# Seven-product f tiles of a SwiGLU half-FFN: three joins moved from VectorE into PSUM banks that ScalarE fills, and each tile's first product issued inside the tile before it

## The chip, the cores and the metric

The kernel is one program on one core of a Trainium2 chip. The metric is device time in microseconds (us) from the program's start to its end. The times of before are 2233.11 us as the median of three runs (2232.19 to 2233.71 us).

Five engines work side by side, each through a queue of its own in fixed order: TensorE (PE in the profile; its weight loads are PEld), VectorE (DVE), ScalarE (ACT), GpSimd (POOL) and SyncE (SP), which here issues nearly all DMAs. Matmuls write into PSUM, an accumulator memory that is used here as eight banks of 512 floats in each of 128 partitions. An engine's instruction that must wait holds up all that is behind it in the same queue.

## What is computed

The reference is one inference step of a two-layer network on 640 tokens (512 latent, 128 context) of width 1024. Each layer is a half-FFN, a token mixer (a Fourier mix in layer 0, attention in layer 1) and another half-FFN, each between norms that are modulated by a conditioning vector:

```python
m = (silu(cond) @ w_mod + b_mod).reshape(9, 1024)        # 9 rows of modulation for each layer
h = rmsnorm(x, g_pre) * (1 + m[3*k + 1]) + m[3*k]
gate, up = split(h @ w1, 2)                               # w1: 1024 x 5632
y = (silu(gate) * up) @ w2                                # w2: 2816 x 1024
x = x + 0.5 * m[3*k + 2] * rmsnorm(y, g_post)
```

There are four half-FFNs, numbered n = 0, 2, 3 and 5 among the six sub-layers. Every float32 product is done as three matmuls on a value split into a coarse part (`hi`) and the rest (`lo`): hi times hi, hi times lo, lo times hi.

## The kernel before

**f tiles.** A half-FFN walks over the 2816 hidden units in 22 tiles of 128, f = 0 to 21. Tile f needs 128 columns of gate weights and 128 columns of up weights over a depth of 1024 (eight chunks of 128), for two halves of the tokens (320 each). Tiles 0 to 3 are done plainly. Tiles 4 to 21 (`w1_fast`) use a scheme with seven products in place of eight blocks: (gate, up) x (first and second half of the depth) x (two token halves). One product is four chunks of three matmuls, 12 matmuls of 128x128 by 320 columns, written by `product`. Four of the seven read sums of activations that `combine` has prepared (`part(1..4)`), and some read sums of weights.

**Banks and joins of one tile.** The products go into four banks: x and y (`score`), z (`turn`) and w (`sum`), in the order x, y, z, w, then a second product on top of x, of z and of w. Between them seven VectorE instructions join the partial results: L715, L718, L722, L728, L729 (times the silu), L733 and L735; ScalarE copies x once (L712) and does the two silus (L725, L734). `hidden` splits each half of the result into hi and lo for the second layer of the FFN.

**Weights.** `unit(i)` hands out the i-th weight unit of a list and first sends every unit up to i + 3. `send` loads a unit by a DMA of 512 KB into a buffer named `raw` (four buffers, shared with everything that is loaded in this shape), then `split` makes hi on ScalarE (L220) and lo on VectorE (L221) in a pool of six pairs. For a fast tile the list has four units: `gate` (loaded), `sums` (the up weights are loaded, and three VectorE adds, L195 to L197, make the sums of gate and up), `up` (from the loaded up weights) and `all` (from the second half of the gate buffer, L203). A gate buffer is so in use until its tile's `all` unit has been split, and an up buffer until its `up` unit has been.

**The w2 stages.** After tiles 4, 8, 12, 16 and 21 a stage multiplies four (at the end six) finished tiles into the output: five token tiles, each 24 matmuls of 512 columns (`w2`). The sums are kept in SBUF between stages, so ScalarE copies each bank out (L781) and the next tile's in (L755). The stage holds its own four weight units to its end.

**Background work.** The modulation rows are matrix-vector products on VectorE: one job loads 512 KB of `w_mod_t` into a `raw` buffer and multiplies it with the two conditioning vectors (`gemv`, two instructions at L429). `behind` takes jobs off a list after each token tile of a w2 stage. `BEHIND` gives 36 jobs to each of n = 0, 2 and 3, which is 9 jobs in each of their four w2 stages, 12 stages in all, and 8 jobs to n = 5.

```python
BEHIND = (36, 12, 36, 36, 0, 8)
...
    def job(layer=layer, idx=idx, f=f):
        j = idx * NCH + f
        self.gemv(self.raw_tile(self.io["w_mod_t"][layer, j]), layer, j)
```

What sets the order on each queue is a scheduler that takes the program's order, priorities and free buffers and writes one fixed list for each engine.

Of the kernel before, what the change touches and what calls it, by code (L numbers as in the profile page):

```python
# [42 lines left out]
FAST = range(4, NF)  # L43
# [83 lines left out]
class Kernel:  # L127
# [54 lines left out]
    def send(self, kind, src):  # L182

        nc, two, one = self.nc, slice(512, UNIT), slice(0, 512)
        at = slice(0, UNIT)
        if kind in ("plain", "block", "gate"):
            raw = self.raw_tile(src)  # L190
            self.fast["gate"] = raw
        elif kind == "sums":
            up, gate = self.raw_tile(src), self.fast["gate"]
            raw = self.raw.tile([P, UNIT], F32, tag="raw", name=self.name("sums"))
            nc.vector.tensor_tensor(raw[:, one], gate[:, one], up[:, one], op=ALU.add)  # L195
            nc.vector.tensor_tensor(up[:, one], up[:, one], up[:, two], op=ALU.add)
            nc.vector.tensor_tensor(raw[:, two], gate[:, one], up[:, one], op=ALU.add)  # L197
# [12 lines left out]
        self.split(hi, lo, raw[:, at])  # L210
        return hi, lo
# [409 lines left out]
    def ffn(self, layer, which, base, boundary):  # L621
# [3 lines left out]
        n = layer * 3 + 2 * which  # L625
        begun = [False, False]
# [7 lines left out]
        def w1(fs, half):  # L634
# [4 lines left out]
            if n == half == 0 and 0 in fs:  # L639
                rest, pss = self.begun  # L640
                for go in rest:
                    go()
            elif len(fs) == 1:
                for f in fs:
                    for j in range(2):
                        with self.behind_of(*[] if n or half else (*self.entered, self.load)):
                            w = self.unit(base + self.w1_at[f] + j)
                        with self.tc.issue_after(self.latest.ins):
                            pss.append(self.proj(w, lambda k: k * P, half, kind="score" if f == 2 and n == 0 else "main"))
            else:  # L650
                pss = self.multi([self.unit(base + self.w1_at[f] + j) for f in fs for j in range(2)], half,
                                 ("main", "main", "turn", "sum"))
# [45 lines left out]
        def product(f, ps, unit, at, x, start):  # L698
            w = self.unit(base + self.w1_at[f] + unit)
# [4 lines left out]
        def w1_fast(f):  # L704

            g[f] = self.ring(F32R).rearrange("p (a t) -> p a t", a=2)
            a, q = (self.temp("left")[:, :HALF] for _ in range(2))
            s, v = (self.temp("right")[:, :HALF] for _ in range(2))
            x, y, z = (self.bank(kind)[:, :HALF] for kind in ("score", "score", "turn"))
            product(f, x, 0, 0, lambda k: self.h.chunk(k, 0), True)  # L710
            with high():
                nc.scalar.activation(a, x, AF.Copy)  # L712
            product(f, y, 1, 512, lambda k: part(2, k), True)
            with high():
                tt(q, y, a, op=ALU.subtract)  # L715
            product(f, z, 1, 0, lambda k: part(3, k), True)
            with high():
                tt(a, q, z, op=ALU.subtract)  # L718
            w = self.bank("sum")[:, :HALF]
            product(f, w, 2, 0, lambda k: part(1, k), True)  # L720
            with high():
                tt(a, a, w, op=ALU.add)  # L722
            product(f, x, 0, 512, lambda k: self.h.chunk(4 + k, 0), False)
            with high():
                nc.scalar.activation(s, x, AF.Silu)  # L725
            product(f, z, 2, 512, lambda k: part(4, k), False)
# [31 lines left out]
        def w2(s, tiles):  # L758
# [7 lines left out]
            for a0, f in [(a, f) for a in range(2) for f in range(f0, f1)] if ends else [(None, f) for f in range(f0, f1)]:  # L766
                w = self.unit(base + self.w2_at[s] + f - f0)
# [20 lines left out]
        for op, a, half in self.ffn_plan:  # L788
# [7 lines left out]
            elif op == "combine":  # L796
                combine(a)
            elif op == "fast":
                w1_fast(a)
# [8 lines left out]
            elif op == "gates":  # L808
                self.gate_rows(n)
                self.gates(n)  # L810
                if n % 3 == 0:
                    self.gate_rows(n + 1)
# [6 lines left out]
    def plan_ffn(self):  # L819

        plan = []
        for half in (0, 1):
            for i, fs in enumerate(((0, 1), (2,), (3,))):
                plan += [("w1", fs, half)]
                if half:
                    plan += [("combine", step, None) for step in ((), (0, 1), (2, 3))[i]]
        due = 0
        for f in FAST:
            if f == NF - 2:
                plan += [("gates", None, None)]  # L830
            plan += [("fast", f, None)]
# [5 lines left out]
        self.ffn_plan = plan  # L837
        self.ffn_units, self.w1_at, self.w2_at = [], {}, {}
        for op, v, half in plan:
            if op == "fast":  # L840
                self.w1_at[v] = len(self.ffn_units)
                self.ffn_units += [("gate", v, 0), ("sums", v, 1)]
                self.ffn_units += [(kind, None, None) for kind in ("up", "all")]
            elif op == "w1":
                for f in v:
                    if f not in self.w1_at:
                        self.w1_at[f] = len(self.ffn_units)
                        self.ffn_units += [("w1", f, 0), ("w1", f, 1)]
            elif op == "w2" and v[0] not in self.w2_at:
                self.w2_at[v[0]] = len(self.ffn_units)  # L850
                f0, f1 = SLICES[v[0]]
                self.ffn_units += [("w2", f0, j) for j in range(f1 - f0)]

    def list_units(self):
        io = self.io
        self.plan_ffn()
        self.bases = []
        for i in range(DEPTH):
            for sub in range(3):
                self.bases.append(len(self.units))  # L860
                if sub != 1:
                    for op, v, j in self.ffn_units:
                        if op == "w2":
                            self.units.append(("plain", io["w2"][i, sub // 2, v + j]))
                        elif op == "w1":
                            self.units.append(("block" if v == 3 else "plain", io["w1"][i, sub // 2, v, j]))
                        else:
                            self.units.append((op, None if v is None else io["w1"][i, sub // 2, v, j]))
# [598 lines left out]
```

## Time and profile before

| | before |
|---|---|
| median of three runs | 2233.11 us |
| profiled execution, its own time | 2233.16 us |
| its span, first to last instruction | 2231.4 us |
| mean granted TensorE clock | 0.996 |
| PE busy | 2198.5 us (99%) |
| DVE busy | 1682.5 us (75%) |
| ACT busy | 1155.6 us (52%) |
| DMA moved | 288.13 MB, mean 129 GB/s |

The page cuts the span into 40 slices: PE is at nine tenths or more in all but the first and the last. So only what makes PE wait can move the end, and the share of the other engines tells little by itself. Waits and the order of the queues have to be read stage by stage.

### The profile page before, as it was taken

The page shows a single profiled execution, that of the slowest core. Times are in us where ns is not written, and L with a number is a line of the kernel's source. Part 1 is how long each engine was busy: PE and PEld are TensorE (multiplying, and loading weights), DVE is VectorE, ACT ScalarE, POOL GpSimd, SP SyncE. Part 2 cuts the span into 40 slices and gives each one's busy share as a digit, 9 for nine tenths or more (in the row PEclk, how much of TensorE's full clock was granted, in tenths as well). Part 3 has the DMA queues.
Part 4 walks back from the last instruction along what each step waited for, and adds up shares of the span by engine and source line. Part 5 has one row for each costly group of instructions (what it writes and reads, how often), then busy time and mean ns, then how long its engine had stood idle before and what let it go on. Part 6 is the DMA issues. An engine that isn't in the chain of part 4 may idle for free. (4 is left out here: it accounts for less than half of the span.)

```text
span 2231.4 us, 35240 instructions
## 1 busy us (share of the span) xinstructions
PE 2198.5 (99%) x13730; PEld 2051.7 (92%) x13730; DVE 1682.5 (75%) x3081; ACT 1155.6 (52%) x2186; POOL 43.7 (2%) x95
## 2 busy tenths in 40 slices
PE   7999999999999999999999999999999999999998
PEld 5999999999899999998999999989999899999997
DVE  5888898687868898887688898776555666766684
ACT  4544454464544454455444554466878644455452
POOL 0000000010000000001000000000000000000000
PEclk8999999999999999999999999999999999999999
DMA  8144444432413444444144344523343322322232
GB/s 313 67 142 161 140 143 144 178 127 94 167 72 123 139 146 149 154 143 178 57 143 150 133 147 150 195 77 105 108 118 111 106 74 95 114 87 88 101 123 104
DMA packets 84424, 288.13 MB, mean 129 GB/s; under 512 B 9537, under 2 KB 14497, under 8 KB 84129
## 3 DMA queue, kind: packets, MB, share of 16 engines
q1 hardware_dynamic: 83712, 285.23, 37.6%
q8 instruction: 107, 1.75, 0.3%
q10 hardware_dynamic: 544, 0.66, 0.1%
q14 instruction: 61, 0.49, 0.1%
HBM read 270.34 MB, written 11.58 MB: 126 GB/s over the span
## 5 line engine op out<-in xcount | busy, mean ns | idle before, releaser
L220 ACT ACTIVATE hi<-raw 128x1024 fp32r<-128x1024 f32 (+1 forms) x374 | 358.4, 973 | 330.2 <-PE score L235 86.9
L221 DVE TENSOR_TENSOR lo<-raw,hi 128x1024 fp32r<-128x1024 f32 (+1 forms) x374 | 416.0, 1118 | 142.1 <-ACT hi L220 140.9
L234 PE MATMUL main<-hi,ring 128*128 128x512 f32 (+2 forms) x1044 | 391.4, 375 | 0.0
L235 PE MATMUL main<-lo,ring 128*128 128x512 f32 (+2 forms) x1044 | 387.8, 372 | 0.8 <-DVE lo L221 0.8
L236 PE MATMUL main<-hi,ring 128*128 128x512 f32 (+2 forms) x1044 | 387.2, 371 | 0.0
L429 DVE SCALAR_TENSOR_TENSOR junk<-raw,wide 128x1024 bf16<-128x1024 f32 x256 | 313.1, 1223 | 95.7 <-DMA raw<-in_w_mod_t 91.3
L236 PE MATMUL score<-ring,lo 128*128 128x320 f32 x896 | 277.1, 309 | 0.3 <-DVE lo L221 0.3
L234 PE MATMUL score<-ring,hi 128*128 128x320 f32 x896 | 277.4, 310 | 0.0
L235 PE MATMUL score<-ring,hi 128*128 128x320 f32 x896 | 276.9, 309 | 0.0
L234 PEld LDWEIGHTS main<-hi,ring 128*128 128x128 f32 x1044 | 196.3, 188 | 34.9 <-issue 1.7
L235 PEld LDWEIGHTS main<-lo,ring 128*128 128x128 f32 x1044 | 196.3, 188 | 33.8 <-DVE lo L221 1.1
L236 PEld LDWEIGHTS main<-hi,ring 128*128 128x128 f32 x1044 | 196.1, 188 | 33.9 <-issue 0.2
L234 PE MATMUL turn<-ring,hi 128*128 128x320 f32 x648 | 200.5, 309 | 2.3 <-DVE left L718 2.1
L236 PE MATMUL sum<-ring,lo 128*128 128x320 f32 x648 | 200.2, 309 | 0.0
L235 PE MATMUL sum<-ring,hi 128*128 128x320 f32 x648 | 200.2, 309 | 0.0
L234 PE MATMUL sum<-ring,hi 128*128 128x320 f32 x648 | 200.2, 309 | 0.0
L235 PE MATMUL turn<-ring,hi 128*128 128x320 f32 x648 | 200.2, 309 | 0.0
L236 PE MATMUL turn<-ring,lo 128*128 128x320 f32 x648 | 200.2, 309 | 0.0
L781 ACT ACTIVATE y<-main 128x512 f32<-128x512 f32 x160 | 94.2, 591 | 200.0 <-PE main L236 199.0
L234 PE MATMUL main<-ring,hi 128*128 128x320 f32 x560 | 181.8, 325 | 1.6 <-ACT ring L220 1.6
L235 PE MATMUL main<-ring,hi 128*128 128x320 f32 x560 | 174.9, 312 | 0.8 <-DVE ring L221 0.8
L236 PE MATMUL main<-ring,lo 128*128 128x320 f32 x560 | 174.8, 312 | 0.0
(247 smaller groups left out, 4371.4 us busy)
## 6 DMA issues: line engine op xcount, KB each, us to landing
raw<-in_w SPq DMA_DIRECT2D x264, 512.0 KB, 3.9
raw<-in_w_mod_t SPq DMA_DIRECT2D x128, 512.0 KB, 3.5
raw<-in_qkv SPq DMA_DIRECT2D x26, 512.0 KB, 3.8
first<-in_w_mod_k SPq DMA_DIRECT2D x16, 512.0 KB, 8.8
spill<-ring SPq DMA_DIRECT2D x12, 640.0 KB, 2.9
ring<-spill SPq DMA_DIRECT2D x12, 640.0 KB, 7.2
raw<-in_bias SPq DMA_DIRECT2D x16, 448.0 KB, 3.8
raw<-in_four_in SPq DMA_DIRECT2D x8, 512.0 KB, 3.8
```

The costliest lines, as they stand in the source:

```text
L220: a = self.nc.scalar.activation(hi, src, AF.Copy)
L221: self.last_split = a, self.nc.vector.tensor_tensor(lo, src, hi.bitcast(F32), op=ALU.subtract)
L234: mm(out, whi, xhi, start=start, stop=False)
L235: mm(out, whi, xlo, start=False, stop=False)
L236: self.latest = mm(out, wlo, xhi, start=False, stop=stop)
L429: last = self.nc.vector.scalar_tensor_tensor(out=self.junk, in0=raw, scalar=1.0, in1=self.wide[:, cond, :], op0=ALU.mult, op1=ALU.mult, ac ...
L781: nc.scalar.activation(place(i, a), ps[a], AF.Copy)
```

## The change

Only `w1_fast`, the list of units and their planning change (`EARLY` is 4, so the branches for another value never run, and `first_half` is never called). Four things are different for tiles 5 to 21 of each half-FFN (tile 4 runs much as before):

- ScalarE puts minus x into bank y before the y product, which then accumulates on top; it copies y into bank w before the w product, which accumulates on top as well; it copies z and y to SBUF. So the joins L715, L718 (in its old place), L722 and L733 become one subtraction (new L765), and four joins are left: L765, L793, L794, L804. ScalarE has six instructions here for three before.
- The tile's products are issued as z, y, second x, w, then the next tile's first x product (`open_fast`), then second z and second w. In tiles 20 and 21 y goes ahead of z.
- The list of units has the next tile's `gate` ahead of this tile's `all`, so the gate weights of a tile are loaded in the tile before it.
- The second of two `gate_rows` calls, each a transposition on PE through bank `turn`, moves from ahead of tile 20 to ahead of tile 21.

```diff
-        elif kind == "sums":
-            up, gate = self.raw_tile(src), self.fast["gate"]
+            if kind == "gate":
+                self.fast["next"] = raw
+        elif kind in ("sums", "again"):
+            self.fast["gate"] = self.raw_tile(src[0]) if kind == "again" else self.fast.pop("next")
+            up, gate = self.raw_tile(src[1]), self.fast["gate"]
...
+        def open_fast(f):
+            if f is None or f in opened:
+                return
+            opened.append(f)
+            product(f, held["x"], "gate", 0, chunk(0, 0), True)
...
+            steps = {
+                "y": lambda: product(f, y, "sums", 512, parts(2), not seeded),
+                "z": lambda: product(f, z, "sums", 0, parts(3), True),
+            }
+            if seeded:
+                with high():
+                    copy(y, x, AF.Copy, scale=-1.0)
+                a, q = left(), left()
+                for step in ("yz" if turned else "zy"):
+                    steps[step]()
+                    with high():
+                        if step == "z":
+                            copy(a, z, AF.Copy)
+                        else:
+                            w = self.bank("sum")[:, :HALF]
+                            copy(w, y, AF.Copy)
+                            copy(q, y, AF.Copy)
+                product(f, x, "gate", 512, chunk(4, 0), False)
+                s, v = right(), q
+                with high():
+                    copy(s, x, AF.Silu)
+                product(f, w, "up", 0, parts(1), False)
+                with high():
+                    tt(a, w, a, op=ALU.subtract)
...
+            open_fast(ahead)
+            product(f, z, "up", 512, parts(4), False)
             with high():
                 tt(v, q, z, op=ALU.subtract)
                 tt(v, v, s, op=ALU.mult)
                 hidden(f, v, 0)
-            product(f, w, 3, 0, lambda k: self.h.chunk(4 + k, 1), False)
+            product(f, w, "all", 0, chunk(4, 1), False)
             with high():
-                nc.vector.scalar_tensor_tensor(out=q, in0=w, scalar=-1.0, in1=q, op0=ALU.mult, op1=ALU.subtract)
-                nc.scalar.activation(q, q, AF.Silu)
+                if seeded:
+                    q = left()
+                    copy(q, w, AF.Silu, scale=-1.0)
                 tt(a, a, q, op=ALU.mult)
                 hidden(f, a, 1)
...
+                need(v, "sums", "again" if again else "sums")
+                need(v, "up")
+                if half[0] is not None:
+                    need(half[0], "gate")
+                need(v, "all")
```

How the queues change is shown at one w2 stage, the second of n = 0, which stands between tiles 8 and 9; the other eleven stages with nine background jobs read alike. First SyncE's loads around the stage, as they stood before. `raw_1769` is the stage's last w2 unit, `raw_1781` and `raw_1793` are gate and up of tile 9, the `in_w_mod_t` rows are the background jobs, and `raw_1995` is the gate of tile 10.

```order
L172 DMA raw_1769<-in_w 128x1024
L172 DMA raw_1781<-in_w 128x1024
L172 DMA raw_1793<-in_w 128x1024
L172 DMA raw_1821<-in_w_mod_t 128x1024
L172 DMA raw_1853<-in_w_mod_t 128x1024
```

Now, on the same queue: `raw_1625` is the gate of tile 9, loaded ahead of the stage's four w2 units, `raw_1792` is the up of tile 9, and `raw_1818` is already the gate of tile 10.

```order
L172 DMA raw_1625<-in_w 128x1024
L172 DMA raw_1700<-in_w 128x1024
L172 DMA raw_1719<-in_w 128x1024
L172 DMA raw_1753<-in_w 128x1024
L172 DMA raw_1780<-in_w 128x1024
L172 DMA raw_1792<-in_w 128x1024
L172 DMA raw_1818<-in_w 128x1024
L172 DMA raw_1832<-in_w_mod_t 128x1024
L172 DMA raw_1864<-in_w_mod_t 128x1024
```

One load more, the gate of tile 10, has moved ahead of the background loads. Next VectorE at the end of the same stage, before. `lo_1810` and `lo_1979` are the `up` and `all` weights of tile 9, which can be split only when the stage's weights come free; L429 are the background jobs, L715 and L718 joins of tile 9.

```order
L429 SCALAR_TENSOR_TENSOR junk,mod<-raw_1929,wide 128x1024
L221 TENSOR_TENSOR lo_1810<-raw_1793,hi_1809 128x1024
L429 SCALAR_TENSOR_TENSOR junk,mod<-raw_1929,wide 128x1024
L442 TENSOR_TENSOR coef<-mod,vec 128x8
L221 TENSOR_TENSOR lo_1979<-raw_1781,hi_1978 128x512
L442 TENSOR_TENSOR coef<-mod,vec 128x8
L429 SCALAR_TENSOR_TENSOR junk,mod<-raw_1961,wide 128x1024 x2
L429 SCALAR_TENSOR_TENSOR junk,mod<-raw_1965,wide 128x1024
L715 TENSOR_TENSOR left_1971<-score_1975,left_1970 128x320
L429 SCALAR_TENSOR_TENSOR junk,mod<-raw_1965,wide 128x1024
L718 TENSOR_TENSOR left_1970<-left_1971,turn_1976 128x320
```

Now, at the same place (`lo_1809` is `up` and `lo_1987` is `all` of tile 9, `lo_1821` the gate of tile 10, L765 a join of tile 9); two more jobs, `raw_1972` and `raw_1976`, come behind the rows shown, and only behind them the adds that make the sums of tile 10.

```order
L431 SCALAR_TENSOR_TENSOR junk,mod<-raw_1900,wide 128x1024
L223 TENSOR_TENSOR lo_1809<-raw_1792,hi_1808 128x1024
L223 TENSOR_TENSOR lo_1821<-raw_1818,hi_1820 128x1024
L431 SCALAR_TENSOR_TENSOR junk,mod<-raw_1900,wide 128x1024
L223 TENSOR_TENSOR lo_1987<-raw_1625,hi_1986 128x512
L431 SCALAR_TENSOR_TENSOR junk,mod<-raw_1904,wide 128x1024 x2
L431 SCALAR_TENSOR_TENSOR junk,mod<-raw_1936,wide 128x1024 x2
L765 TENSOR_TENSOR left_1983<-sum_2015,left_1983 128x320
L431 SCALAR_TENSOR_TENSOR junk,mod<-raw_1940,wide 128x1024 x2
L444 TENSOR_TENSOR coef<-mod,vec 128x8 x2
```

Of the stage's 18 background instructions 5 stood behind the `up` split of tile 9 before; now 11 do. Last PE where tile 10 first needs its sums (`hi_2034`, `lo_2035` before). Before, that is the y product, behind the first x product (`score_2106`):

```order
L234 MATMUL score_2106<-ring_212,hi_1997 128x320
L235 MATMUL score_2106<-ring_213,hi_1997 128x320
L236 MATMUL score_2106<-ring_212,lo_1998 128x320
L234 MATMUL score_2107<-ring_824,hi_2034 128x320
L235 MATMUL score_2107<-ring_825,hi_2034 128x320
L236 MATMUL score_2107<-ring_824,lo_2035 128x320
```

Now the sums (`hi_2038`, `lo_2039`) are needed by the z product (`turn_2111`), behind the second x product (`score_910`), and the y product (`score_911`) is woven into it:

```order
L236 MATMUL score_910<-ring_336,hi_1820 128x320
L237 MATMUL score_910<-ring_337,hi_1820 128x320
L238 MATMUL score_910<-ring_336,lo_1821 128x320
L236 MATMUL turn_2111<-ring_893,hi_2038 128x320
L237 MATMUL turn_2111<-ring_894,hi_2038 128x320
L236 MATMUL score_911<-ring_824,hi_2038 128x320
L237 MATMUL score_911<-ring_825,hi_2038 128x320
L238 MATMUL turn_2111<-ring_893,lo_2039 128x320
```

From the end of the stage to this point PE has eight products before (seven of tile 9 and the first x of tile 10) and eight now (z, y, second x and w of tile 9, the first x of tile 10, second z and second w of tile 9, the second x of tile 10).

More of the change, by code (lines that the diff above doesn't have):

```diff
@@ L650, in w1 @@
             else:
-                pss = self.multi([self.unit(base + self.w1_at[f] + j) for f in fs for j in range(2)], half,
+                pss = self.multi([self.unit(base + w1_at[f, kind]) for f in fs for kind in ("gate", "up")], half,
                                  ("main", "main", "turn", "sum"))
@@ new lines, in ffn, with first_half @@
+        chunk = lambda c, half: lambda k: self.h.chunk(c + k, half)
+        parts = lambda i: lambda k: part(i, k)
+        copy = nc.scalar.activation
+        stash, held, opened = {}, {}, []
+        def first_half(fs):
+            room = self.ring(F32).rearrange("p (i t) -> p i t", t=HALF)
+            pss = [self.bank()[:, :HALF] for _ in fs]
+            stash.update({f: (room[:, 2 * i], room[:, 2 * i + 1]) for i, f in enumerate(fs)})
+            for i, f in enumerate(fs):
+                product(f, pss[i], "gate", 0, chunk(0, 0), True)
+                with high():
+                    copy(stash[f][0], pss[i], AF.Copy)
+            for i, f in enumerate(fs):
+                product(f, pss[i], "gate", 512, chunk(4, 0), False)
+                with high():
+                    copy(stash[f][1], pss[i], AF.Silu)
@@ new lines, in open_fast, with w1_fast @@
+        def open_fast(f):
[3 more added lines that the diff above has]
+            product(f, held["x"], "gate", 0, chunk(0, 0), True)
+        def w1_fast(f, ahead, turned):
+            g[f] = self.ring(F32R).rearrange("p (a t) -> p a t", a=2)
+            if not held:
+                held.update({kind: self.bank("score")[:, :HALF] for kind in "xy"})
+            seeded = bool(opened)
+            x, y = held["x"], held["y"]
+            z = self.bank("turn")[:, :HALF]
+            left, right = (lambda kind=kind: self.temp(kind)[:, :HALF] for kind in ("left", "right"))
+            steps = {
[17 more added lines that the diff above has]
+                s, v = right(), q
+                with high():
+                    copy(s, x, AF.Silu)
+                product(f, w, "up", 0, parts(1), False)
+                with high():
+                    tt(a, w, a, op=ALU.subtract)
+            else:
+                if f in stash:
+                    b, s = stash.pop(f)
+                else:
+                    open_fast(f)
+                    b, s = left(), right()
+                    with high():
+                        copy(b, x, AF.Copy)
+                q = left()
+                steps["y"]()
+                with high():
+                    tt(q, y, b, op=ALU.subtract)
+                steps["z"]()
+                a, v = left(), right()
+                with high():
+                    tt(a, q, z, op=ALU.subtract)
+                w = self.bank("sum")[:, :HALF]
+                product(f, w, "up", 0, parts(1), True)
+                with high():
+                    tt(a, a, w, op=ALU.add)
+                if opened:
+                    product(f, x, "gate", 512, chunk(4, 0), False)
+                    with high():
+                        copy(s, x, AF.Silu)
+            open_fast(ahead)
+            product(f, z, "up", 512, parts(4), False)
```

116 lines of the change are left out of this document (60 added, 56 removed).

## The prediction

> **What bounds the kernel now.** I read the page first, busy shares and slices, then the list of waits by length, then the windows around a w2 stage, and last the timelines of VectorE and PE there.
>
> ```profile
> PE 2198.5 (99%) x13730; PEld 2051.7 (92%) x13730; DVE 1682.5 (75%) x3081; ACT 1155.6 (52%) x2186; POOL 43.7 (2%) x95
> ```
>
> PE is busy for 2198.5 of 2231.4 us, and the change leaves the number of matmuls as it is. So it can only win what PE waits today, and lose what PE will wait. The waits in the seven-product tiles are these:
>
> ```profile
> PE turn L538 <- ACT rms L540: 2.7, 2, 1.5
> PE turn L234 <- DVE left L718: 2.1, 2, 1.4
> PE score L236 <- DVE lo L221: 0.3, 1, 0.3
> ```
>
> L538 is the transposition of `gate_rows`, L718 a join, the third the split of a tile's sums. Together 5.1 us: that is all the change can gain, 0.2% of the span. What it can lose stands in the tightest place of a half-FFN, the w2 stage with background jobs and the four tiles behind it (window: busy time of PE, PEld, DVE, ACT, POOL, then clock):
>
> ```profile
> 181.80:209.00 27.20, 27.20 (x122) 22.54 (x121) 21.63 (x36) 13.72 (x23) 0.00 (x0) 1.00 0.43 146
> 209.00:258.30 49.30, 49.30 (x337) 49.26 (x337) 46.83 (x77) 24.59 (x38) 0.00 (x0) 1.00 0.43 144
> ```
>
> PE fills both windows, but VectorE is at 46.83 of 49.30 us behind the stage: it has hardly any room to work off a backlog. Nine jobs, 18 background instructions (each with a short read, so two records), fall to this place:
>
> ```profile
> 181.80:209.00 27.20, 16.01 (x26) 1.00 0.43 146
> 209.00:221.40 12.40, 6.14 (x10) 1.00 0.56 190
> ```
>
> That is L429 alone: 13 of 18 run inside the stage, 5 behind it.
>
> **Part 1, the joins.** 68 tiles (17 in each of four half-FFNs) lose three VectorE instructions each and gain three ScalarE copies.
>
> ```profile
> L728 DVE TENSOR_TENSOR right<-left,turn 128x320 f32<-128x320 f32 x72 | 34.7, 482 | 4.2 <-PE turn L236 4.1
> L712 ACT ACTIVATE left<-score 128x320 f32<-128x320 f32 x72 | 31.0, 430 | 10.3 <-PE score L236 9.3
> ```
>
> VectorE: 204 x 0.482 = 98 us less. ScalarE: 204 x 0.430 = 88 us more; in four tiles 12 x 0.43 = 5.2 on top of 24.6 of 49.3, so there is room. Neither shortens PE's own work; both are worth only the waits above, at most the 2.1 of L718. No row of before shows a 320-column copy into PSUM at a join; the nearest, of 512 columns, take 602 ns into PSUM and 591 out of it, so I price it as the 0.43 out.
>
> ```profile
> L755 ACT ACTIVATE main<-y 128x512 f32<-128x512 f32 x146 | 87.6, 602 | 15.3 <-DVE ring L583 11.0
> L781 ACT ACTIVATE y<-main 128x512 f32<-128x512 f32 x160 | 94.2, 591 | 200.0 <-PE main L236 199.0
> ```
>
> The copy into bank y has z's product in front of it, the copy into w the second x product, so nearly all are covered. A product is 12 matmuls at a pitch of 0.147 us, 1.76 us:
>
> ```profile
> 302.00 0.31 PE L234 MATMUL turn<-ring,hi 128*128 128x320 f32 x1
> 302.15 0.31 PE L235 MATMUL turn<-ring,hi 128*128 128x320 f32 x1
> ```
>
> Where that cover fails is rival two. Behind the last join, L793 to L804, stand 1.76 us of PE's next product: 0 for each tile, 0.6 at most.
>
> **Part 2, the gate unit loaded a tile earlier.** This is where I expect the time to go. Of four `raw` buffers, before, two are held through the stage (gate and up of tile 9) and two circulate for the jobs. Now gate 9, up 9 and gate 10 are all loaded ahead of the jobs and all held, since up 9 cannot be split before the stage's weights leave the pool and gate 10 stays until its `all`. One buffer is left: each job's load must wait for the second L429 (L431 now) of the job before it. What such a round costs is seen on VectorE:
>
> ```profile
> 188.42 0.08 DVE L429 DVE_READ_ACCUMULATOR junk<-raw,wide 128x1 f32 x1
> ...
> 192.07 1.23 DVE L429 SCALAR_TENSOR_TENSOR junk<-raw,wide 128x1024 bf16<-128x1024 f32 x1 [2.97 <-DMA raw<-in_w_mod_t]
> ...
> 194.61 1.23 DVE L429 SCALAR_TENSOR_TENSOR junk<-raw,wide 128x1024 bf16<-128x1024 f32 x1
> ...
> 197.03 0.08 DVE L429 DVE_READ_ACCUMULATOR junk<-raw,wide 128x1 f32 x1
> ...
> 200.82 1.23 DVE L429 SCALAR_TENSOR_TENSOR junk<-raw,wide 128x1024 bf16<-128x1024 f32 x1
> ```
>
> The job that reads until 188.50 frees a buffer whose next content is read from 192.07: 3.57 us. Again 197.11 to 200.82: 3.71. So a round is 3.65, and a job's two instructions 2.54 (192.07 to 194.61), together 6.2 us for each job, where two buffers gave 13 instructions in the stage.
>
> In us from the stage's start (181.8), the length 27.2 as before. The split of the sums of tile 9, which has to come first, waits for PE's last product, some 0.8 later than its 183.78 today; the first load goes at 4.0, so the first four jobs start at 7.65, 13.85, 20.05 and 26.25. In VectorE's list the first half of the fourth job ends at 27.5; then follow the splits of up 9 and gate 10 (28.65 and 29.8), the fourth job's second half (31.1) and the half split of `all` (31.7). These free three buffers at 28.7, 31.1 and 31.7, and jobs 5, 6, 7 have data 3.65 later, 32.3, 34.8, 35.4. From 32.3 VectorE is full: five jobs x 2.54 = 12.7, four joins 1.6, coefficients 0.2, two ring splits 0.8 (by L728's spacing of 0.4). The last background instruction ends at **47.5**; before, at 34.7:
>
> ```profile
> 183.78 1.22 DVE L221 TENSOR_TENSOR lo<-sums,hi 128x1024 fp32r<-128x1024 f32 x1
> ...
> 216.41 0.08 DVE L429 DVE_READ_ACCUMULATOR junk<-raw,wide 128x1 f32 x1
> ...
> 218.03 0.69 DVE L195 TENSOR_TENSOR sums<-raw,raw 128x512 f32<-128x512 f32 x1
> ...
> 219.75 0.69 DVE L197 TENSOR_TENSOR sums<-raw,raw 128x512 f32<-128x512 f32 x1
> ...
> 221.57 1.23 DVE L221 TENSOR_TENSOR lo<-sums,hi 128x1024 fp32r<-128x1024 f32 x1 [0.40 <-ACT hi L220]
> ...
> 223.11 1.22 DVE L221 TENSOR_TENSOR lo<-raw,hi 128x1024 fp32r<-128x1024 f32 x1
> ```
>
> All 18 stand in VectorE's list ahead of the adds of tile 10's sums: three adds 2.1 (49.6), hi on ScalarE 1.06 (50.7), lo 1.22 (51.95).
>
> ```profile
> L220 ACT ACTIVATE hi<-sums 128x1024 fp32r<-128x1024 f32 x72 | 76.4, 1061 | 123.7 <-DVE sums L197 111.5 <-PE sum L235 10.0 <-DVE right L728 1.4
> ```
>
> PE has eight products to its first matmul on these sums: 27.2 + 8 x 1.76 + 0.2 for a join = 41.5. It waits 50.7 - 41.5 = **9.2 us**, and 0.1 more for lo. Before, its y product stood at 41.3 with lo ready at 41.0 (222.8): the margin was 0.3, so the backlog is paid in full. Queued behind the waiting matmul is PE's whole list, so nothing covers it.
>
> **The clock after such a wait.** The last matmul of the program starts at 2224.67; the clock reads 1.00 for 3.6 us and 0.50 behind. At the start the long wait ends at 35.94 with the clock at 0.50 until 41:
>
> ```profile
> 2224.67 0.39 PE L236 MATMUL main<-hi,ring 128*128 128x512 f32 x1
> 2225.20:2228.80 3.60, 0.00 (x0) 0.00 (x0) 2.18 (x4) 0.64 (x2) 0.54 (x1) 1.00 0.12 46
> 2229.00:2231.40 2.40, 0.00 (x0) 0.00 (x0) 0.00 (x0) 0.00 (x0) 0.00 (x0) 0.50 0.32 119
> 35.94 0.64 PE L234 MATMUL main<-ring,hi 128*128 128x320 f32 x1
> 37.17 0.47 PE L235 MATMUL main<-ring,hi 128*128 128x320 f32 x1
> 37.44 0.47 PE L236 MATMUL main<-ring,lo 128*128 128x320 f32 x1
> 34.20:40.90 6.70, 6.05 (x31) 5.17 (x28) 2.00 (x8) 2.09 (x6) 0.00 (x0) 0.50 1.03 378
> 41.00:47.00 6.00, 6.00 (x43) 6.00 (x43) 3.93 (x11) 5.97 (x9) 0.00 (x0) 1.00 0.75 304
> ```
>
> So a wait of 9.2 us, over 3.7, drops the clock, and PE then runs about 5.0 us (35.94 to 41) at a pitch of 0.267 in place of 0.147: 5.0 x (1 - 0.147/0.267) = 2.25 us lost.
>
> The Trainium skill ("TensorE: Matmul & The Clock Gate", section "The HAM clock gate") has the clock fall after an idle window of about 3.4 us and rise again after about 3.4 us of busy time. By that figure, an estimate, a stall would lose 1.5 us, and the sum be 2358. The rows agree with the fall (3.7 us) and show a longer way back (5.0).
>
> **The sum.** 9.2 + 2.25 + 0.1 = 11.6 us for a stage. The same list stands at all 12 stages with nine jobs (four each in n = 0, 2, 3): 139 us. The four stages of n = 5 have two jobs each, done by 7.65 + 6.2 + 2.54 = 16.4 with the stage still running, and cost nothing. Less the 5.1 of waits that go: +134. The profiled execution took 2233.16 us, 1.8 over its span and equal to the median of 2233.11: 2233 + 134 = **2367 us**.
>
> Bounds for a stage. Low: a round of 3.3 instead of 3.65 (the loads land in 3.5 by the page's median, part of a round) ends the jobs 1.7 earlier; with joins and splits lying inside the waits for data, 1.6 earlier again; no clock loss: 5.9, so 12 x 5.9 - 5 = +66, 2299.
>
> ```profile
> raw<-in_w_mod_t SPq DMA_DIRECT2D x128, 512.0 KB, 3.5
> ```
>
> High: first load 2 us later, half clock through all 6.7 us of its window (3.0), 0.7 of backlog left for tile 11: 9.2 + 2 + 3.0 + 0.7 = 14.9, less 5: +174, 2407.
>
> **The rivals.** *As aimed* (6%): the jobs keep pace, so that no new wait comes and all 5.1 us go: 2228. It decides by whether nine jobs still end by about 34.7. For it speaks that VectorE has 98 us less to do; against it that those are 1.2 us for a tile, while the loop through one buffer lacks 12.8.
>
> *The copies into bank w come late, and the backlog doesn't* (9%): in the second tile behind each of 16 stages only four matmuls (0.59 us) lie between the y product's end and the w product. The copy needs 0.16 for the last matmul's end (0.31 long at a pitch of 0.147) and 0.43, 0.59 in all, so just enough, or up to 1.06 more when a hi split is ahead on ScalarE. 16 x 0 to 1.06 = 0 to 17 us, less 5: 2228 to 2245. It needs the jobs to end in time, like the first.
>
> *The backlog is handed on* (4%): VectorE's spare 2.5 us behind a stage don't absorb what remains, so that tiles 11 and 12 wait as well: over 2407.
>
> That the change does not do what it says is excluded by the lists: the three joins are gone and the gate load stands ahead.
>
> **How the numbers follow.** The backlog has 81%, of it nearly all between its bounds. The range is 2299 to 2407; both small rivals and the long one are left out. 0.2% (4.5 us) is about what a measurement of this kernel tells from no change. Faster is the first rival and the near end of the second, 0.07; same is most of what is left of the second, 0.05; slower the rest, 0.88.
>
> **What would show it.** The background instructions wait for DMA before nearly every job in the stages; PE waits about 9 us, 12 times, in the second tile behind a stage (tiles 6, 10, 14, 18) at bank `turn` for hi of the sums; the clock reads below 1.00 just behind it; the four tiles behind a stage take 61 us, not 49.3; VectorE's busy time falls by some 98 us. Wrong it would be if these waits are absent, if two loads of `w_mod_t` overlap in a stage, or if n = 5 loses as much as n = 0.

## The result, and the profile after

The changed kernel takes 2359.92 us (median of five runs, 2357.02 to 2363.33) against 2233.11 us before: a ratio of 1.0568, 95% interval 1.0553 to 1.0584. The prediction was 2367 us, with a range of 2299 to 2407. The profiled execution has a span of 2359.5 us, 128.1 more than before.

The page of the changed kernel, the row of busy times (microseconds, share of the span, instructions), then of the 40 slices PE's busy tenths and its clock:

```profile
PE 2232.1 (95%) x13730; PEld 2075.4 (88%) x13730; DVE 1608.9 (68%) x2877; ACT 1225.3 (52%) x2390; POOL 43.7 (2%) x95
PE   7989889899999889889998898899999999999998
PEclk8999999999999999999999999999999999999999
```

VectorE does 73.6 us less, ScalarE 69.7 more, PE has the same 13730 matmuls and is busy 33.6 us longer. The slices at 8 show that PE now waits in the first two thirds, where n = 0, 2 and 3 lie. The list of waits names the place (what waited and for what; us in total, times, longest). First VectorE's loads before, then the changed kernel:

```profile
DVE junk L429 <- DMA raw<-in_w_mod_t: 91.3, 54, 3.7
```

```profile
DVE junk L431 <- DMA raw<-in_w_mod_t: 208.9, 75, 4.5
PE turn L236 <- ACT hi L222: 98.3, 12, 8.6
PE turn L540 <- DVE left L793: 1.0, 1, 1.0
PE turn L236 <- DVE left L793: 0.7, 1, 0.7
```

Twelve waits of 8.2 us in the mean, on the split of a tile's sums, at bank `turn`; and the background instructions waited 208.9 us for their loads, where they had waited 91.3. The row names ScalarE, since its hi came last; what held hi up is found by following VectorE back. PE's other idle time is 3.8 us shorter on balance (2231.4 - 2198.5 = 32.9 us before, 2359.5 - 2232.1 - 98.3 = 29.1 now): 98.3 + 33.6 - 3.8 = 128.1.

VectorE's timeline at the second w2 stage of n = 0, which starts at 194.6 in this run (start, length, engine and line, tiles; in brackets the idle time before and what ended it):

```profile
202.00 1.22 DVE L431 SCALAR_TENSOR_TENSOR junk<-raw,wide 128x1024 bf16<-128x1024 f32 x1 [3.12 <-DMA raw<-in_w_mod_t]
...
208.03 1.23 DVE L431 SCALAR_TENSOR_TENSOR junk<-raw,wide 128x1024 bf16<-128x1024 f32 x1 [3.54 <-DMA raw<-in_w_mod_t]
...
214.05 1.23 DVE L431 SCALAR_TENSOR_TENSOR junk<-raw,wide 128x1024 bf16<-128x1024 f32 x1 [3.51 <-DMA raw<-in_w_mod_t]
...
220.19 1.23 DVE L431 SCALAR_TENSOR_TENSOR junk<-raw,wide 128x1024 bf16<-128x1024 f32 x1 [3.64 <-DMA raw<-in_w_mod_t]
...
241.60 0.08 DVE L431 DVE_READ_ACCUMULATOR junk<-raw,wide 128x1 f32 x1
241.60 0.68 DVE L197 TENSOR_TENSOR sums<-raw,raw 128x512 f32<-128x512 f32 x1
...
244.85 1.22 DVE L223 TENSOR_TENSOR lo<-sums,hi 128x1024 fp32r<-128x1024 f32 x1 [0.40 <-ACT hi L222]
```

That is one job each 6.0 us, with a wait of 3.5 us for the load before each: one buffer goes round. The sums of tile 10 (L197) come right behind the last background instruction. The same time on PE: the stage and the four tiles behind it as two windows (busy time of PE, PEld, DVE, ACT, POOL; the clock), then PE alone in three parts of the second:

```profile
194.60:221.80 27.20, 27.20 (x122) 22.54 (x121) 13.29 (x22) 14.61 (x24) 0.00 (x0) 1.00 0.32 97
221.80:282.80 61.00, 52.45 (x337) 51.35 (x337) 50.22 (x78) 28.01 (x49) 0.00 (x0) 0.92 0.41 138
```

```profile
236.40:244.80 8.40, 0.00 (x0) 0.69 0.32 112
244.90:249.70 4.80, 4.80 (x17) 0.50 0.34 109
249.80:282.80 33.00, 33.00 (x224) 1.00 0.38 128
```

PE stands still for 8.4 us, then works 4.8 us at half clock: 17 matmuls in 4.8 us, which take 17 x 0.147 = 2.5 at full clock, so 2.3 us are lost. The four tiles take 61.0 us, not 49.3. This stage has the longest of the twelve waits; the shortest is 7.2 us.

| us from the stage's start | predicted | this stage |
|---|---|---|
| first job has its data | 7.65 | 7.4 |
| one round of the buffer | 6.2 | 6.0, 6.0, 6.1 |
| last background instruction ends | 47.5 | 47.1 |
| PE comes to the sums | 41.5 | 41.7 |
| hi of the sums is there | 50.7 | 50.3 |
| PE's wait (mean of the twelve) | 9.2 | 8.6 (8.2) |
| lost at half clock | 2.25 | 2.3 |
| stage and four tiles, more than before | 11.6 | 88.2 - 76.5 = 11.7 |

### The profile page after: what moved, and what is told of

Same layout as the page of the kernel before. It is cut to its first block, busy times and chain, and to the rows that moved or that the text cites. A ratio compares the mean times of both kernels' runs of the same rounds, so it can differ in the third digit from the quotient of the medians.

```text
span 2359.5 us, 35252 instructions
## 1 busy us (share of the span) xinstructions
PE 2232.1 (95%) x13730; PEld 2075.4 (88%) x13730; DVE 1608.9 (68%) x2877; ACT 1225.3 (52%) x2390; POOL 43.7 (2%) x95
## 5 line engine op out<-in xcount | busy, mean ns | idle before, releaser
L431 DVE SCALAR_TENSOR_TENSOR junk<-raw,wide 128x1024 bf16<-128x1024 f32 x256 | 313.0, 1222 | 212.5 <-DMA raw<-in_w_mod_t 208.9
L236 PE MATMUL turn<-ring,hi 128*128 128x320 f32 x648 | 210.3, 325 | 99.0 <-ACT hi L222 98.3
L236 PE MATMUL score<-ring,hi 128*128 128x320 f32 x896 | 281.6, 314 | 0.0
L237 PE MATMUL score<-ring,hi 128*128 128x320 f32 x896 | 280.2, 313 | 0.0
L236 PEld LDWEIGHTS turn<-ring,hi 128*128 128x128 f32 x648 | 127.7, 197 | 104.2 <-ACT hi L222 101.4
L238 PE MATMUL turn<-ring,lo 128*128 128x320 f32 x648 | 208.8, 322 | 0.0
L237 PE MATMUL turn<-ring,hi 128*128 128x320 f32 x648 | 207.3, 320 | 0.0
```

Source lines behind the costliest of these rows:

```text
L236: mm(out, whi, xhi, start=start, stop=False)
L237: mm(out, whi, xlo, start=False, stop=False)
L238: self.latest = mm(out, wlo, xhi, start=False, stop=stop)
L431: last = self.nc.vector.scalar_tensor_tensor(out=self.junk, in0=raw, scalar=1.0, in1=self.wide[:, cond, :], op0=ALU.mult, op1=ALU.mult, ac ...
```

## The experiments

The theory: gate 10 held through the stage leaves one buffer for the jobs' loads, so they end late, and the sums stand behind them in VectorE's list. The rivals: ScalarE's three added copies make hi late (it is ScalarE that the row names); VectorE's list or its sheer work decides, whatever the buffers.

**One half of the change at a time.** First the new joins without the early gate and first product:

```diff
-            seeded = bool(opened)
+            seeded = True
             if seeded:
+                open_fast(f)
...
-            ahead = f + 1 if f + 1 < NF and (early == 4 or f > 2) else None
+            ahead = None
```

> The new joins (six ScalarE copies, four VectorE joins) in all fast tiles, but each tile's first product stays in its own tile, and the next gate unit behind the `all` unit, as before. Theory (one raw buffer circulates in the w2 stages because the next gate is held through them): two buffers circulate again, no wait of PE on hi of the sums above 1 us, span within 2226 to 2245 us (ratio 0.997 to 1.006). Rival J (the trace names ScalarE's hi as the releaser: its three added copies per tile make it late): about as slow as the changed kernel, 2340 to 2370 us, with 12 waits near 8 us.

Measured: 2250.42 us, ratio 1.0079 (1.0066 to 1.0091). The values that this kernel returns differ from the reference's. By this edit tile 4 too accumulates on what ScalarE put into its bank, which may be why but wasn't shown; instructions and sizes are as in the other tiles. Next the early gate and first product with the old joins:

```diff
-            seeded = bool(opened)
+            seeded = False
```

> The old joins (VectorE again) in all fast tiles, but the next tile's first product and gate unit stay early. Theory: the 12 waits stay; three more VectorE joins of 0.4 us stand in the backlog, so each wait is 8.2 + 1.2 = 9.4 us, and the time about 2360 + 14 = 2374 us (2355 to 2390). Rival J (ScalarE's copies): near before, 2228 to 2245 us.

Measured: 2354.39 us, ratio 1.0542 (1.0528 to 1.0556). The first row is PE's largest wait in total in the fast tiles with the joins alone, the second with the order alone:

```profile
PE sum L236 <- ACT sum L758: 7.8, 14, 1.4
```

```profile
PE score L236 <- ACT hi L222: 89.3, 12, 8.8
```

The twelve waits come with the order alone and go with the joins alone. So it isn't ScalarE's copies, though the row names its hi. The wait is 7.4 us, not the 9.4 expected: that the old joins would lengthen the backlog is refuted, and the time lies just below its range. The joins alone cost 17 us, above the 2226 to 2245 given to them: something more is in them, taken up below.

**The buffers alone.** In the changed kernel, the tile behind a stage doesn't open the next one, so that no gate is held through a stage and the three other gates of four stay early:

```diff
-            seeded = bool(opened)
+            seeded = f in opened
...
-            ahead = f + 1 if f + 1 < NF and (early == 4 or f > 2) else None
+            ahead = f + 1 if f + 1 < NF and f not in (5, 9, 13, 17) else None
```

> The changed kernel, but in the first tile behind each w2 stage (tiles 5, 9, 13, 17) the next tile is not opened early, so the gate of tiles 6, 10, 14, 18 is loaded behind `all`; those tiles have the old joins, the other 13 of 17 are as changed. Theory: three of four gates move early still, but none is held through a stage, so two buffers circulate: the 12 waits go, 2226 to 2245 us. Rival J: the copies remain in 52 of 68 tiles, so about 2233 + 127 x 52/68 = 2330 us. Rival V (the jobs are ahead of the sums in VectorE's list, whatever the buffers, and PE comes to the sums no sooner than before): here the list and PE's place are nearly those of before, so V gives about 2233 too and is told apart by the next kernel.

And in the kernel before, with nothing moved, one buffer less:

```diff
-NRAW = 4
+NRAW = 3
```

> The kernel before, unchanged but for three raw buffers in place of four. Theory: gate and up of the tile behind the stage are held and one buffer circulates, as in the changed kernel; the last background instruction ends some 12 us later than before, PE waits 8 to 11 us at 12 places (score, for hi or lo of the sums of the second tile behind a stage), clock below 1.00 behind each: at least 2340 us, about 2233 + 12 x (10 + 2.8) = 2387 us. Rival V (the place of the jobs in VectorE's list, not the buffers): 2225 to 2250 us.

Measured: 2249.98 us (ratio 1.0074, 1.0061 to 1.0088) and 2398.51 us (1.0740, 1.0726 to 1.0755). VectorE at the second stage, with the late gate (stage from 183.9), then before with three buffers (from 193.9):

```profile
191.16 1.22 DVE L431 SCALAR_TENSOR_TENSOR junk<-raw,wide 128x1024 bf16<-128x1024 f32 x1 [0.41 <-DMA raw<-in_w_mod_t]
...
194.40 1.23 DVE L431 SCALAR_TENSOR_TENSOR junk<-raw,wide 128x1024 bf16<-128x1024 f32 x1 [0.74 <-DMA raw<-in_w_mod_t]
...
197.27 1.23 DVE L431 SCALAR_TENSOR_TENSOR junk<-raw,wide 128x1024 bf16<-128x1024 f32 x1 [0.37 <-DMA raw<-in_w_mod_t]
```

```profile
206.57 1.23 DVE L429 SCALAR_TENSOR_TENSOR junk<-raw,wide 128x1024 bf16<-128x1024 f32 x1 [3.40 <-DMA raw<-in_w_mod_t]
...
212.52 1.23 DVE L429 SCALAR_TENSOR_TENSOR junk<-raw,wide 128x1024 bf16<-128x1024 f32 x1 [3.44 <-DMA raw<-in_w_mod_t]
...
218.57 1.23 DVE L429 SCALAR_TENSOR_TENSOR junk<-raw,wide 128x1024 bf16<-128x1024 f32 x1 [3.56 <-DMA raw<-in_w_mod_t]
```

With two buffers a job comes each 3 us, with one each 6. The late gate's time, too, is above the 2226 to 2245 expected: 17 us over before, like the joins alone. PE's waits for the sums in the kernel before with three buffers:

```profile
PE score L234 <- ACT hi L220: 72.4, 17, 8.4
PE score L236 <- DVE lo L221: 24.8, 13, 3.3
```

The old kernel gets the same illness from one missing buffer, and the changed one is rid of it with the gate later. The late gate also holds back the first product and the new joins of the second tile, so it can't tell these three apart by itself; the order alone has the waits without the new joins, and the three buffers have them with nothing moved. That settles the cause: the buffers, with neither the joins nor the product order needed for it. With three buffers one is missing in every phase, not in the stages alone; PE waits for hi in 17 places, not 12, and the time is above the 2387 us expected. Whether a fifth buffer would cure it wasn't tried.

**The jobs.** Without loads, then fewer of them in a stage:

```diff
-                        self.gemv(self.raw_tile(self.io["w_mod_t"][layer, j]), layer, j)
+                        self.gemv(self.wide[:, 0, :], layer, j)
```

> The changed kernel, but every background job multiplies the conditioning vector by itself in place of a loaded row block: the same 256 VectorE instructions, no load and no raw buffer for them (so the modulation rows have other values). Theory (the jobs are late because each load waits for the one free buffer): all 18 instructions of a stage run without a gap, 18 x 1.27 = 23 us, done inside the stage; the 12 waits of 8 us and the low clock go. What is left is the second cost seen in the first group of runs, the copies into bank w: 2240 to 2262 us. Rival A (VectorE has too much to do behind a stage, loads or not): the waits stay, above 2330 us.

```diff
                 w1_fast(a, *half)
+                if BEHIND[n] == 36 and 5 <= a <= 20:
+                    self.behind(1)
...
-                    due = BEHIND[n] * passed // (TILES * end)
+                    due = passed if BEHIND[n] == 36 else BEHIND[n] * passed // (TILES * end)
```

> The changed kernel with five jobs in each of the 12 stages in place of nine (one behind each token tile), and one behind each of the 16 fast tiles 5 to 20. Theory: through one buffer four jobs fit in the stage at 6.2 us each and the fifth ends at about 35 us, so the sums of the second tile are ready near 40.5, just ahead of PE at 41.5: the 8 us waits fall below 1.5 us, the clock stays 1.00; the jobs in the tiles take a buffer from the gates, which may cost up to 1 us a tile: 2245 to 2295 us. Rival A (VectorE's total work behind a stage decides): the work only moves by a tile, so the wait stays above 5 us: above 2310 us.

Measured: 2232.22 us without loads (0.9993, 0.9984 to 1.0002), and 2251.56 us with the jobs spread (1.0084, 1.0064 to 1.0105). The twelve waits are gone in both. Without loads the time is below the 2240 to 2262 expected, as the jobs did more than the expectation said: bound to no buffer, they were set ahead into every gap of VectorE, so that by 800 us all of them are done (the last window of the span, L431 alone: VectorE's busy time and instructions):

```profile
800.00:2231.00 1431.00, 0.00 (x0) 1.00 0.30 98
```

So this run shows that the jobs make the backlog, but can't tell their loads from their place; the late gate and the three buffers do that, where the jobs load and stand in the stages as before. The spread kernel adds that through one buffer five jobs a stage keep pace, where nine don't; its time is as expected, though its clock didn't stay at 1.00 everywhere (last section). The control, the kernel before with the same edit:

> The kernel before with the same edit as in the changed kernel without loads: the background jobs multiply the conditioning vector by itself, and load nothing (other modulation values). It is the control to that run (2232 us): what is the change worth where no job needs a raw buffer? If the three joins put into PSUM and the early first product are worth something, this kernel is slower than 2232 us by more than the waits of 2.1 + 2.7 + 0.3 us allow, say 2235 to 2240 us; if they are worth nothing, as PE had next to no waits there, it is at 2227 to 2234 us.

Measured: 2227.24 us, ratio 0.9969 (0.9957 to 0.9981). Its interval lies below that of the changed kernel without loads: even with no loads of jobs in its way the change is worth less than nothing, by some 5 us.

**The clock.** Added matmuls keep PE busy during the wait, first 40, then 52:

```diff
+                if n in (0, 2, 3) and f in (6, 10, 14, 18):
+                    hi = self.unit(base + w1_at[f, "gate"])[0][:, :P]
+                    for _ in range(40):
+                        with self.tc.issue_after(self.latest.ins):
+                            nc.tensor.matmul(banks[0][:, :HALF], hi, self.h.chunk(0, 0)[0], start=True, stop=True)
```

> The changed kernel with 40 added matmuls of 128x128 by 320 columns, 40 x 0.147 = 5.9 us of extra PE work, into an idle bank ahead of the second x product of the second tile behind each of the 12 stages (tiles 6, 10, 14, 18; their result is overwritten, the output is the same). Theory (8.2 us of wait and 2.8 us of half clock behind it for each stage): the wait left is 8.2 - 5.9 = 2.3 us, too short for the clock to fall, so the clock stays 1.00 and the time falls by 12 x 2.8 = 34 us to about 2326 us (2318 to 2336), though PE has 70 us more to do. Rival B (the 33 us by which PE's busy time grew are not the clock but slower matmuls behind a stall, such as weight loads): 2350 to 2365 us.

Measured: 2358.15 us, ratio 1.0550 (1.0534 to 1.0567). The added matmuls changed the values of one output, contrary to the expectation. What was expected of the time failed. PE's waits for the sums, and windows of 8 us behind two of them (PE's busy time, then the clock):

```profile
PE turn L236 <- ACT hi L222: 28.8, 12, 2.8
```

```profile
245.15:253.15 8.00, 7.60 (x38) 0.79 0.40 131
1043.23:1051.23 8.00, 7.60 (x48) 1.00 0.42 131
```

Waits of 2.4 us in the mean were left, and yet the clock fell behind ten of the twelve (0.79 to 0.81; the expectation of the next run says all, which these windows correct): 0.79 over 8 us is 3.4 us at half. Around the first of the two, where PE waits from 242.46 to 245.15:

```profile
242.50:246.80 4.30, 1.25 (x6) 1.00 0.41 122
246.80:250.20 3.40, 3.40 (x15) 0.51 0.48 154
```

The clock falls 1.7 us after PE has resumed. So the run didn't separate wait and clock, and that its time lies in the range of rival B decides nothing. Again with 52, in bank `turn`:

```diff
+                warm = n in (0, 2, 3) and f in (6, 10, 14, 18)
+                if warm:
+                    product(f, x, "gate", 512, chunk(4, 0), False)
+                    hi = self.unit(base + w1_at[f, "gate"])[0][:, :P]
+                    for _ in range(52):
+                        with self.tc.issue_after(self.latest.ins):
+                            nc.tensor.matmul(z, hi, self.h.chunk(0, 0)[0], start=True, stop=True)
...
-                product(f, x, "gate", 512, chunk(4, 0), False)
+                if not warm:
+                    product(f, x, "gate", 512, chunk(4, 0), False)
```

> The changed kernel with 52 added matmuls of 320 columns (52 x 0.147 = 7.6 us) into bank `turn` in the 12 second tiles, between the second x product and the z product that overwrites them (the second x product is issued ahead of them, as the changed kernel's queue has it). The run with 40 left waits of 1.5 to 2.9 us, and the clock fell behind all of them, against what was expected; here 8.2 - 7.6 = 0.6 us of wait is left. Theory (the half clock behind the stalls, 24 us of lost pitch in the changed kernel, is a cost of its own): the clock stays 1.00 behind the 12 places and the time falls to 2360 - 24 = 2336 us (2330 to 2342), with 92 us more work on PE. Rival B (the stall itself or the product behind it costs this, not idleness): 2352 to 2362 us.

Measured: 2353.26 us, ratio 1.0532 (1.0518 to 1.0546). PE behind the added matmuls:

```profile
244.60:250.20 5.60, 4.61 (x30) 1.00 0.37 141
```

```profile
245.71 0.31 PE L237 MATMUL turn<-ring,hi 128*128 128x320 f32 x1
246.72 0.41 PE L238 MATMUL turn<-ring,lo 128*128 128x320 f32 x1 [0.70 <-DVE lo L223]
```

The clock stays at 1.00, yet only 7 us are won, not 24. The added matmuls don't lengthen the stall: with the short waits ahead of and behind them they take 91.7 + 3.1 + 3.4 = 98.2 us in all, as long as PE stood still before (98.3). The second fence shows one reason: at full speed PE comes sooner to the lo of the sums, which VectorE ends at its own time, and waits 0.70 us there. These waits sum to 8.3 us, and the joins behind them add more:

```profile
PE turn L238 <- DVE lo L223: 8.3, 12, 0.7
PE sum L236 <- DVE left L773: 3.2, 5, 1.3
PE turn L236 <- DVE left L801: 3.0, 9, 1.1
```

The theory missed. The time lies in rival B's range, and the product behind the stall does cost something; but that the low clock has no price of its own isn't borne out: without the added 624 x 0.147 = 91.7 us, PE's busy time is 2305.4 - 91.7 = 2213.7 us, 18.4 less than in the changed kernel, and some 12 us of new waits take most of that back. The half clock is real, but most of it lies beside VectorE's backlog and costs about 7 us net.

**The other 17 us.** Three attempts at a version without the backlog and without the waits that the joins bring. With the late gate, y goes ahead of z, to give the copy into w two products of cover:

```diff
-                for step in ("yz" if turned else "zy"):
+                for step in "yz":
```

> As the kernel with the late gate (tiles 6, 10, 14, 18 not opened early), and in all opened tiles the y product goes ahead of z, so that two products, z and second x, stand between y and w. Theory of the second cost (PE waits at bank `sum` for ScalarE's copy of y into w, 8.0 us in 12 waits over 0.3 us in that kernel, since the second x product alone did not cover it): these waits go, the waits for the VectorE subtraction ahead of the second w product (4.0 us) stay: 2250 - 8 = 2242 us (2236 to 2246). Rival C (the 17 us are spread over PE by the changed order and not in these waits): 2248 to 2253 us.

On top of it, in tiles 5, 9, 13 and 17, the w product goes ahead of the second x product:

```diff
+                if ahead is None and not turned:
+                    product(f, w, "up", 0, parts(1), False)
+                    with high():
+                        tt(a, w, a, op=ALU.subtract)
                 product(f, x, "gate", 512, chunk(4, 0), False)
...
-                product(f, w, "up", 0, parts(1), False)
+                if ahead is not None or turned:
+                    product(f, w, "up", 0, parts(1), False)
```

> As the late-gate kernel with y first, and in the tiles that do not open the next one (5, 9, 13, 17) the w product goes ahead of the second x product, so that two products, not one, stand between w and the second w product, which waited 14.1 us in 12 waits for the VectorE subtraction that reads bank `sum`. Theory: these waits go: 2249 - 14 = 2235 us (2230 to 2241). Rival C (the wait moves on to another join): above 2244 us.

And the spread jobs with y first (the edits of both):

> As the spread kernel (five jobs in a stage, one behind each fast tile, all gates early, all new joins), and y ahead of z in all opened tiles. In the spread kernel PE waited 14.6 us at z for the VectorE join that reads bank `turn` before it (one product between) and 5.5 us at w for ScalarE's copy; with y first two products lie between in both places. Theory: both go: 2252 - 20 = 2232 us (2226 to 2240). Rival C (VectorE is late by whole job instructions, and the wait only moves to the next join, as from z-first to y-first with the late gate): 2245 to 2253 us.

Measured: 2248.93 us (1.0068, 1.0056 to 1.0081), 2253.24 us (1.0081, 1.0068 to 1.0095) and 2250.10 us (1.0070, 1.0056 to 1.0084). All three miss their theory, and lie where their rivals C put them. PE's waits in the fast tiles, with the late gate, then with y first, then with w first:

```profile
PE sum L236 <- ACT sum L757: 8.0, 12, 1.9
PE sum L236 <- DVE left L765: 4.0, 10, 0.9
```

```profile
PE sum L236 <- DVE left L765: 14.1, 12, 1.7
```

```profile
PE score L236 <- ACT right L794: 18.0, 12, 2.0
```

The wait does not go, it goes on: from the copy into w to the subtraction that reads w, and from there to the silu that reads x in the second tile, which the next tile's first product waits for. ScalarE at that place, with w first:

```profile
235.96 1.06 ACT L222 ACTIVATE hi<-sums 128x1024 fp32r<-128x1024 f32 x1 [4.47 <-DVE sums L199]
236.92 1.99 ACT L222 ACTIVATE hi<-raw 128x1024 fp32r<-128x1024 f32 x2
238.82 0.42 ACT L794 ACTIVATE right<-score 128x320 f32<-128x320 f32 x1
```

The silu (L794) stands behind three splits, which began only when VectorE had the sums: each engine's fixed queue hands the delay to the next. With the late gate it is the rival C of the second attempt that holds. The rival of the first, that the 17 us lie elsewhere, does not: counted from start to start (0.147 us where PE doesn't wait), the matmuls that open a product in bank `sum` come more than 0.35 us late in 20 places with the late gate, 14.9 us in all, and in no place before; that is most of the 16.1 us by which its span is longer. In the spread kernel the waits of 14.6 and 5.5 us did go, but many of under 0.7 us came in their place, and the time stayed. Those two sums are from its slowest execution (2259.85 us; the other three took 2248.51 to 2251.86), so they are likely too large for the median. None of these versions beats the kernel before.

## Why the prediction was right

**What bounds the kernel**: right. PE has next to no waits before, and only new ones could move the time.

**Part 1, the joins**: right that VectorE's relief is worth nothing; VectorE's busy time fell by 73.6 us rather than 98, since neighbouring instructions overlap (joins of 0.48 us start 0.40 apart). Too kind on their cost: I had 0 a tile, and in the second rival 2228 to 2245 once the backlog is away. The kernels without the backlog whose jobs still load stand at 2249 to 2253. The term missed is that a copy or join that PE waits for may have splits or adds ahead of it on ScalarE or VectorE (three splits, 3 us, in the fence with w first), at more places than bank w of the second tile.

**Part 2, the buffer**: right in mechanism and size. The late gate removes the twelve waits, the missing buffer makes them in the old kernel, and the first five times of the table are within 0.5 us of the trace. The wait was 8.2 us in the mean against 9.2: the round is 6.0 us, not 6.2, and so the last job ends earlier (the prediction's own terms add to 47.6, not 47.5, for its end).

**The clock**: the half clock behind each stall is there, 2.25 us forecast and 2.3 lost in the stage shown. As what the clock costs it is too large: with the clock kept up, 7 us of the whole came back and not 12 x 2.25 = 27. While PE is slow, VectorE works on what PE would wait for next; I had counted the backlog as paid with the one wait for hi and 0.1 for lo, and it isn't. So the sum of +134 us, against +128.1 of the span, is right with the wait 1 us a stage too long (12 us in all) and some small waits behind it left out (PE's busy time grew by 33.6 us, not by 28): the two errors offset each other in part, and that part is luck. And a wait needn't reach the 3.7 us that I took for the limit (last section).

**n = 5 and the gains**: no wait of this sort stands in n = 5; twelve places, as forecast. Of the 5.1 us of old waits, rows of 1.0 and 0.7 us are left.

**The page on the clock**: the Trainium skill ("TensorE: Matmul & The Clock Gate", section "The HAM clock gate") was weighed with 3.4 us idle and 3.4 us back. The stall of 8.4 us shown kept PE at half clock for 4.8 us, nearer to the 5.0 of the start; behind the waits of 2.4 us it was 3.4, the page's figure, but those waits are shorter than the idle window that it asks for; in the traces 3.4 us is the step at which the clock changes (last section), and it fell behind steps in which PE was busy for two fifths of the time.

## What to carry to other kernels

A load that is moved earlier holds its buffer longer: count, at the tightest stage, how many buffers of the pool are still free to go round, and what the round trip then makes of everything that uses them. A wait's row names the last link (here ScalarE's hi); follow the in-order queue behind it to the first instruction that waits for something outside. And before relieving an engine, see whether anyone waits for it: here VectorE lost 73.6 us of work and the time grew by 5.7%.

## What the runs showed of the hardware

The clock fell after waits much shorter than the prediction took for its limit (3.7 us), and while PE was at work again. No wait length parts the cases: in the run with 40 added matmuls it held behind a wait of 2.45 us, and in the spread kernel it fell behind one that was shorter:

```profile
1043.23 0.42 PE L236 MATMUL turn<-ring,hi 128*128 128x320 f32 x1 [2.45 <-ACT hi L222]
```

```profile
227.73 0.39 PE L236 MATMUL turn<-ring,hi 128*128 128x320 f32 x1 [1.95 <-DVE left L793]
```

The traces do hold what parts them. In all fourteen profiled executions every change of the clock lies on a grid: any two changes are a whole number of steps of 3.41 us apart. These are the steps around the two waits, each with PE's busy time and then the clock, first for the wait at which the clock held:

```profile
1038.77:1042.18 3.41, 2.01 (x14) 1.00 0.21 47
1042.19:1045.60 3.41, 1.97 (x11) 1.00 0.41 115
```

```profile
225.03:228.44 3.41, 1.46 (x11) 1.00 0.71 190
228.45:231.85 3.40, 3.40 (x15) 0.50 0.30 119
```

The longer wait is shared by two steps, in which PE is still busy for 0.59 and 0.58 of the time. The shorter one falls into a single step, whose busy share is 0.43 with the end of the product before, and the next step runs at half clock. Counted over all fourteen traces, the clock fell behind every step at full clock with a busy share below 0.43 and behind none above 0.58; between the two both are found. So it is how a wait falls into the steps that decides, and a wait of 2 us can do what one of 2.45 us doesn't.
